# A two-layer decoder step: cache pages loaded one by one from SyncE, and half of the key products in three fp32r passes

## The chip, the core and the metric

The kernel runs on one core of a Trainium2 chip. The core has TensorE (matmuls into PSUM), VectorE, ScalarE and GpSimd, SyncE as a queue that issues transfers, and 16 DMA engines between DRAM and SBUF. The metric is the device time in microseconds of one execution. In the profile TensorE is PE (PEld its weight loads), VectorE DVE, ScalarE ACT, GpSimd POOL and SyncE SP.

## What is computed

One inference step of a decoder with two layers, for a prompt of 1024 tokens and a sample group of 8 sequences with 4 new tokens each. Every layer norms and projects its input, runs three branches (a pooling mixer, a short convolution and latent attention), gates them and projects back. The change touches the sample group's attention over its cache, 64 pages of 128 tokens for each sequence, found through a page table:

```
def step(carry, pt):
    m, lsum, acc = carry
    lat = cache_latent[layer, pt]            # (8, 128 tokens, 128 channels)
    krp = cache_krope[layer, pt]             # (8, 128 tokens, 32)
    kn = key_nope(lat, w_uk, kn_g)           # rmsnorm of (lat @ w_uk), 4 heads x 64
    s = attn_scores(qn, qr, kn, krp)
    m_new = jnp.maximum(m, jnp.max(s, axis=-1))
    corr = jnp.exp(m - m_new)
    p = jnp.exp(s - m_new[..., None])
    lsum = lsum * corr + jnp.sum(p, axis=-1)
    acc = acc * corr[..., None] + jnp.einsum('bhqk,bkc->bhqc', p, lat.astype(jnp.float32))
    return (m_new, lsum, acc), None
```

## The kernel before

Each layer has three stages. The projections with the preparation of queries and keys come first, then the cache stage, then the prompt's attention, whose first tiles overlap the end of the cache stage; the output projection follows. The first is ordered by a scheduler, the cache stage and the prompt's attention in the order in which the code writes them.

The cache stage (`sample_attn`, L481) goes over 16 units, each half of one sequence's pages: 32 pages, 4096 tokens. A unit has 8 steps of 512 tokens (`tau` counts all 128 steps). Both layouts of a unit's pages come by indirect gathers from GpSimd (`rows`, L490): `latc` for the keys, two units ahead, `lat` for the values, and the rotary keys `kr`. VectorE turns 512 columns of `latc` a step, in blocks of 32, three steps ahead (`T`, L519). `K` (L529) is the key product: for each of four groups of 128 tokens one fp32 matmul of the turned block with `WK`, 272 columns wide: 256 key channels for the norms and 16 score columns, into which the queries are folded. In the program an fp32 matmul is one row; on the chip it is two instructions. ScalarE squares the 256 columns and copies the 16 (`nope`, L545); each `kproj` buffer in PSUM (there are three, of two groups each) is free when both have read it. GpSimd adds the halves of the squares (`tree`), VectorE sums them (`red`), and per unit the inverse root (`lnexp`, `newton`), the scaling, the rotary part, the maximum, the exponential and the value product `pv` (L614) follow, one and two units behind.

Of the 8 buffers of the pool `big` (`slot`, L58) the stage uses those that the gate rows `mixM` and `mixA` of the prompt and the prompt's first head leave. In layer 0, seven blocks of `w_ada` for later modulation are loaded whole beside the units (`ada_step`, L630). In the prompt's attention, `load_qk` and `load_v` (L816, L822) fetch one head from DRAM, and `qk_part` and `v_part` split it into two fp32r parts on ScalarE and GpSimd; `warm` (L846) does that for head 0 in the last units. A product in three passes is `mm3` (L213): high by high, high by low, low by high, each an fp32r matmul with its own weights.

## Time and profile before

| | us |
|---|---|
| three runs, median | 1607.45 |
| lowest and highest | 1606.56, 1608.36 |
| the profiled execution's own time | 1606.35 |
| its span, first to last instruction | 1604.6 |
| TensorE busy | 1547.2 (96%) |
| VectorE busy | 1122.6 (70%) |
| ScalarE busy | 790.4 (49%) |
| GpSimd busy | 743.8 (46%) |

The busy times are sums over the whole span; a stretch is read from its own rows. A matmul's recorded duration holds its way through the array, and neighbours overlap, so the distance of two starts is what a matmul takes in a row of them. SyncE's transfers are not counted as busy; their rows in order of time show the issue alone, and the data land later.

### The profile page before, as it was taken

To read this page: it belongs to the slowest core of one execution; us is meant where nothing else is said; L and a number is where in the kernel's file an instruction comes from. 1 tells how busy PE (TensorE), PEld (TensorE's weight loads), DVE (VectorE), ACT (ScalarE), POOL (GpSimd) and SP (SyncE) were. 2 spreads that over 40 slices of the span, in tenths; PEclk is the share of its full clock that TensorE was granted. 3 is DMA by queue.
4 is the path that set the end of the run, shared out by engine and by line. 5 is a ranking of instruction groups with operands and counts; after the bars stand their busy time and mean duration, and the time that the engine had idled before them with its cause. 6 is when DMAs were issued, how large, how long until landed. Compare 5 with 4: busy or idle time off the path is not lost.

```text
span 1604.6 us, 28029 instructions
## 1 busy us (share of the span) xinstructions
PE 1547.2 (96%) x10576; PEld 1386.7 (86%) x10576; DVE 1122.6 (70%) x2131; ACT 790.4 (49%) x1935; POOL 743.8 (46%) x594
## 2 busy tenths in 40 slices
PE   4899999999999999999998999999999999989999
PEld 2799999977777888889987999998888888878999
DVE  7746755578888888684268477546899999967522
ACT  4444444365555556583145344334666665657500
POOL 3311211276666667364444021223777777746520
PEclk8999999999999999999999999999999999999999
DMA  9202223567777775213522112314666666541242
GB/s 385 56 20 70 64 77 73 171 273 281 297 285 281 287 272 192 59 47 121 202 90 70 41 40 73 78 60 153 243 260 260 261 261 251 206 125 48 68 160 82
DMA packets 79557, 254.48 MB, mean 159 GB/s; under 512 B 25472, under 2 KB 49088, under 8 KB 69184
## 3 DMA queue, kind: packets, MB, share of 16 engines
q0 software_dynamic: 13824, 151.00, 23.7%
q1 hardware_dynamic: 65600, 101.69, 20.0%
q8 instruction: 85, 1.39, 0.3%
q14 instruction: 48, 0.39, 0.1%
HBM read 231.87 MB, written 20.80 MB: 157 GB/s over the span
## 4 chain that ended last, share of the span: by engine, by line
PE 87%; DVE 6%; DMA 2%; issue 2%; ACT 1%; POOL 1%; SPq 0%; DVEq 0%; POOLq 0%; ACTq 0%
PE kproj L541 29%; PE po L620 4%; PE ropesc L569 3%; PE outa L198 2%; PE outa L200 2%; PE outa L196 2%; PE PTp L166 2%; PE rawps L216 2%; PE rawps L214 2%; PE rawps L215 2%; PE pvo L214 1%; DMA src<-qscr 1%; PE outb L200 1%; PE outb L196 1%; PE outb L198 1%
## 5 line engine op out<-in xcount | busy, mean ns | idle before, releaser
L541 PE MATMUL kproj<-WK,lT 128*128 128x272 f32 x2048 | 497.5, 397 | 3.9 <-DVE lT L525 3.9
L541 PEld LDWEIGHTS kproj<-WK,lT 128*128 128x128 f32 x2048 | 378.9, 190 | 90.0 <-issue 15.9
L101 ACT ACTIVATE sq<-kproj 128x512 f32<-128x512 f32 x512 | 305.3, 597 | 252.0 <-PE kproj L541 248.9
L104 POOL TENSOR_TENSOR t<-sq 128x512 f32<-128x512 f32 x256 | 322.3, 1274 | 138.3 <-ACT nope L547 108.3
L104 POOL TENSOR_TENSOR wt<-wraw,wt 128x1024 fp32r<-128x1024 f32 x44 | 106.9, 2431 | 312.4 <-ACT wt L116 308.3
L525 DVE STREAM_TRANSPOSE lT<-latc 128x512 f32<-128x512 f32 x256 | 177.4, 694 | 35.7 <-PE kproj L541 31.9
L557 DVE TENSOR_REDUCE ms<-t 128x16 f32<-128x512 f32 x256 | 167.0, 652 | 10.8 <-POOL t L104 10.5
L116 ACT CAST wt<-wraw 128x1024 fp32r<-128x1024 f32 x44 | 46.7, 1064 | 125.1 <-PE outb L200 81.2
L547 ACT COPY nope<-kproj 128x32 f32<-128x32 f32 x512 | 93.0, 182 | 0.6 <-DMA qscr<-qkm 0.6
L104 POOL TENSOR_TENSOR kn<-raw,ones 128x128 f32<-128x128 f32 x18 | 13.0, 723 | 163.6 <-DVE raw L104 88.2
L1365 PE MATMUL zma<-hT,wt 128*128 128x352 f32 x192 | 49.9, 366 | 26.8 <-ACT hT L1145 18.9
L569 PEld LDWEIGHTS ropesc<-BD,krT 128*128 128x128 f32 x512 | 66.8, 192 | 4.7
L886 DVE TENSOR_REDUCE pmx<-sc 128x1 f32<-128x128 f32 (+3 forms) x64 | 48.1, 751 | 26.7 <-PE pvo L166 23.5
L1365 PEld LDWEIGHTS zma<-hT,wt 128*128 128x128 f32 x192 | 36.9, 214 | 33.6 <-ACT hT L1145 21.6
L104 DVE TENSOR_TENSOR PT<-PTp,PT 128x512 fp32r<-128x512 f32 (+2 forms) x96 | 50.2, 551 | 21.8 <-ACT PT L929 20.8
L929 ACT CAST PT<-PTp 128x512 fp32r<-128x512 f32 (+2 forms) x96 | 42.8, 481 | 45.9 <-PE PTp L166 45.4
L569 PE MATMUL ropesc<-BD,krT 128*128 128x64 f32 x512 | 64.0, 268 | 0.0
L620 PE MATMUL po<-lat,p 128*32 128x128 f32 x2048 | 62.5, 274 | 0.0
L104 POOL TENSOR_TENSOR qkT<-src,qkT 96x512 fp32r<-96x512 f32 x32 | 40.9, 1279 | 33.6 <-ACT qkT L832 33.3
L620 PEld LDWEIGHTS po<-lat,p 128*32 128x32 f32 x2048 | 53.9, 110 | 2.1
L104 POOL TENSOR_TENSOR nope<-nope,rs 128x512 f32<-128x512 f32 x32 | 35.2, 1100 | 35.2 <-DVE rs L581 35.2
L101 ACT ACTIVATE P<-sc,pmx 128x128 f32<-128x128 f32 (+3 forms) x64 | 47.9, 749 | 6.9 <-DVE pmx L886 6.3
(452 smaller groups left out, 3906.2 us busy)
## 6 DMA issues: line engine op xcount, KB each, us to landing
wada<-in_w_ada SPq DMA_DIRECT2D x11, 2048.0 KB, 8.0
wraw<-in_w_in SPq DMA_DIRECT2D x32, 512.0 KB, 3.8
wraw<-in_w_out SPq DMA_DIRECT2D x14, 512.0 KB, 5.1
qscr<-qkm SPq DMA_DIRECT2D x32, 192.0 KB, 2.1
xo<-in_xT SPq DMA_DIRECT2D x8, 528.0 KB, 5.3
xscr<-xn SPq DMA_DIRECT2D x8, 528.0 KB, 3.0
xo<-xscr SPq DMA_DIRECT2D x8, 528.0 KB, 5.6
vscr<-Vm SPq DMA_DIRECT2D x16, 256.0 KB, 2.0
```

The costliest lines, as they stand in the source:

```text
L101: s.activation(out, in_, func, **k)
L104: (e or v).tensor_tensor(out, x, y, op)
L196: te.matmul(outs[n], wt[:, 0, k, :], hi[:, n * CH:(n + 1) * CH], start=(k == 0), stop=False)
L198: te.matmul(outs[n], wt[:, 0, k, :], lo[:, n * CH:(n + 1) * CH], start=False, stop=False)
L200: te.matmul(outs[n], wt[:, 1, k, :], hi[:, n * CH:(n + 1) * CH], start=False, stop=(k == 7))
L525: v.transpose(h.lT[q], h.latc[:, 512 * q:512 * q + 512])
L541: te.matmul(kp[:, i, 0:KPC], lT[:, sl], wk, start=True, stop=True)
L547: s.copy(h.nope[:, t0:t0 + 2].rearrange("p n h t -> p n (h t)"), kp[:, :, 256:KPC])
L557: v.tensor_reduce(h.ms[:, 4 * q:4 * q + 4, :].rearrange("p n (h o) -> p (n h) o", o=1), t32, AX.X, ALU.add)
L569: te.matmul(h.pr[:, o:o + 64], h.krT[c][:, 128 * k:128 * k + 128], BD[:, h.b, :], start=True, stop=True)
L620: te.matmul(h.po[32 * j:32 * j + 32, 0:128], p[:, 16 * t:16 * t + 32], h.lat[:, t * 128:(t + 1) * 128], start=(q == 0), stop=(q == 7))
L1365: te.matmul(o, zmw[j][:, i // 2, k, :], (lo if i == 1 else hi)[:, c], start=(k == 0 and i == 0), stop=(k == 7 and i == 1))
```

## The change

Pages no longer come by gathers of a whole unit. `pages(tau)` issues four transfers on SyncE, each one page of 128 rows of 1 KB: 128 numbers of the page by channels (the layout that the key product wants as weights) and 128 by tokens (the layout for the values), which the host has laid side by side in DRAM. The page's number comes from the table `pgt` in SBUF into a register of SyncE, eight numbers in one instruction every second step, and a further instruction multiplies it to an address. The transposes `T` and the gathers of `latc` and `lat` are gone; the gather of `kr` stays, in another order of rows. In steps 1, 3, 5 and 7 of a unit ScalarE and GpSimd split the block into two fp32r parts (`cast`, three steps ahead) and the key product runs as `mm3`. In these steps the squares are summed by VectorE alone, from the full width; in the others VectorE copies the 16 score columns instead of ScalarE. `newton` runs on GpSimd, with one square on ScalarE. Pages are issued five steps ahead, in buffers of 16 pages. To free buffers, the gate rows `mixM` and `mixA` go to DRAM (`mscr`) after the projections and come back during the prompt's attention. `w_ada` comes in eight pieces, one a step. Head 0's value split moves behind the stage, and the splits of head 1 come one tile later.

```
-    WKR = cp.tile([128, 2, 256], F32R, name="WKR")
-    WK = [cp.tile([128, KPC], F32, name=f"WK{i}") for i in range(2)]
+    pgt = cp.tile([1, 2 * NB * 32], I32, name="pgt")
+    WUK = cp.tile([128, 2, KPC], F32R, name="WUK")
...
+    NTAU = NU * NSTEP
+    THREE = (1, 3, 5, 7)
+    AHEAD, CAST = 5, 3
...
+        krs, sums = [], []
+        numbers = []
+
+        def pages(tau):
+
+            if tau >= NTAU:
+                return
+            u, q = divmod(tau, NSTEP)
+            if q == 0:
+                H[u] = P()
+                H[u].b, H[u].pg = u // 2, []
             h = H[u]
-            h.lat = flat(slot(f"lat{l}_{u}"), 4096)
-            rows(u, h.lat, "lat")
+            if q % 4 == 0:
+                h.pg.append(flat(slot(f"pg{l}_{u}_{q}"), 4096).rearrange("p (n x) -> p n x", n=16))
+            if q % 2 == 0:
+                _, values = nc.values_load_multi_w_load_instructions(
+                    pgt[0:1, 4 * tau:4 * tau + 8], engines=[mybir.EngineType.SP], min_val=0, max_val=NPOOL - 1,
+                    skip_runtime_bounds_check_because="entries of the page table are numbers of pages of the pool")
+                numbers[:] = values
+            for i in range(4):
+                nc.sync.dma_start(h.pg[q // 4][:, 4 * (q % 4) + i, :],
+                                  a["pages"][l][bass.ds(numbers.pop(0), 1)].rearrange("o p x -> p (o x)"))
...
+        def turned(h, q):
+            return h.pg[q // 4][:, 4 * (q % 4):4 * (q % 4) + 4, 0:128]
+
+        def cast(tau):
+            u, q = divmod(tau, NSTEP)
+            if tau < NTAU and q in THREE:
+                h = H[u]
+                h.hl = getattr(h, "hl", {})
+                hi = pool.tile([128, 4, 128], F32R, tag="hi", name="hi", bufs=3)
+                lo = pool.tile([128, 4, 128], F32R, tag="lo", name="lo", bufs=3)
+                s.copy(hi, turned(h, q))
+                sub(lo, turned(h, q), f(hi), g)
+                h.hl[q] = hi, lo
...
             for i in range(2):
                 t = 2 * j + i
-                sl = slice(t * 128, (t + 1) * 128)
-                te.matmul(kp[:, i, 0:KPC], lT[:, sl], wk, start=True, stop=True)
+                if q in THREE:
+                    hi, lo = h.hl[q]
+                    mm3(kp[:, i, 0:KPC], hi[:, t], lo[:, t], wr[:, 0], wr[:, 1])
+                else:
+                    te.matmul(kp[:, i, 0:KPC], turned(h, q)[:, t], wk, start=True, stop=True)
+            if q in THREE and j:
+                h.hl.pop(q)
             act(h.sq[:, 2 * j:2 * j + 2, :], kp[:, :, 0:256], AF.Square)
             return kp
...
         def nope(h, q, j, kp):
             t0 = 4 * q + 2 * j
-            s.copy(h.nope[:, t0:t0 + 2].rearrange("p n h t -> p n (h t)"), kp[:, :, 256:KPC])
-
-        def tree(h, q):
-            sv = h.sq.rearrange("p n (h x d) -> p (n h) x d", h=NH, x=2)
-            t32 = pool.tile([128, 16, 32], F32, tag="t32", name="t32", bufs=3)
-            add(t32, sv[:, :, 0, :], sv[:, :, 1, :], g)
-            halves.append((h, q, t32))
+            dst = h.nope[:, t0:t0 + 2].rearrange("p n h t -> p n (h t)")
+            if q in THREE:
+                s.copy(dst, kp[:, :, 256:KPC])
+            else:
+                v.tensor_copy(dst, kp[:, :, 256:KPC])
+
+        def add_up(h, q):
+
+            x = h.sq.rearrange("p n (h d) -> p (n h) d", h=NH)
+            if q not in THREE:
+                t32 = pool.tile([128, 16, 32], F32, tag="t32", name="t32", bufs=2)
+                add(t32, x[:, :, 0:32], x[:, :, 32:64], g)
+                x = t32
+            sums.append((h, q, x))
 
         def red():
-            h, q, t32 = halves.pop(0)
-            v.tensor_reduce(h.ms[:, 4 * q:4 * q + 4, :].rearrange("p n (h o) -> p (n h) o", o=1), t32, AX.X, ALU.add)
+            h, q, x = sums.pop(0)
+            v.tensor_reduce(h.ms[:, 4 * q:4 * q + 4, :].rearrange("p n (h o) -> p (n h) o", o=1), x, AX.X, ALU.add)
 
...
         def lnexp(h):
             h.t0 = keep.tile([128, 32, NH], F32, tag="ta", name="ta", bufs=2)
+            h.rs = keep.tile([128, 32, NH], F32, tag="rs", name="rs", bufs=2)
             act(h.t0, h.ms, AF.Ln, scale=1.0 / NOPE, bias=epsT)
             act(h.t0, h.t0, AF.Exp, scale=-0.5)
-
-        def newton(h):
-            h.rs = keep.tile([128, 32, NH], F32, tag="rs", name="rs", bufs=2)
-            mul(h.rs, h.t0, h.t0)
-            v.tensor_scalar(h.ms, h.ms, -0.5 / NOPE, -0.5 * EPS, ALU.mult, ALU.add)
-            mul(h.rs, h.rs, h.ms)
-            v.scalar_tensor_tensor(h.rs, h.rs, 1.5, h.t0, ALU.add, ALU.mult)
+            act(h.rs, h.t0, AF.Square)
+
+        def newton(h, e=g):
+            e.tensor_scalar(h.ms, h.ms, -0.5 / NOPE, -0.5 * EPS, ALU.mult, ALU.add)
+            mul(h.rs, h.rs, h.ms, e)
+            if e is v:
+                v.scalar_tensor_tensor(h.rs, h.rs, 1.5, h.t0, ALU.add, ALU.mult)
+            else:
+                e.tensor_scalar_add(h.rs, h.rs, 1.5)
+                mul(h.rs, h.rs, h.t0, e)
...
             if not odd:
-                if q == 3:
-                    A.w = ada_load(*ada[c])
+                if q == 0:
+                    A.w = flat(slot(f"wada{c}"), 4096).rearrange("p (k n) -> p k n", k=8)
+                nc.sync.dma_start(A.w[:, q], a["w_ada"][ada[c]][:, q])
...
+        for tau in range(AHEAD):
+            pages(tau)
         gather_kr(0)
-        gather_kr(1)
+        add(WK[0][:, 0:256], f(WUK[:, 0, 0:256]), f(WUK[:, 1, 0:256]))
+        v.tensor_copy(WK[1][:, 0:256], WK[0][:, 0:256])
+        v.tensor_copy(WKR[1][:, :, 0:256], f(WUK[:, :, 0:256]))
         new_wk(0)
-        T(0)
-        T(1)
-        T(2)
+        for tau in range(CAST):
+            cast(tau)
...
-            T(tau + 3)
+            pages(tau + AHEAD)
             kp = K(h, q, 0)
+            cast(tau + CAST)
             nope(h, q, 0, kp)
-            if tau > 1:
+            if q % 2 == 0 and sums:
                 red()
...
             kp = K(h, q, 1)
-            tree(h, q)
+            add_up(h, q)
             nope(h, q, 1, kp)
+            if q % 2:
+                red()
             if hp is not None:
                 if q == 1:
-                    lnexp(hp)
+                    newton(hp)
...
-                elif q == 3:
+                elif q == 1:
                     rowsum(hpp, u - 2)
+                elif q == 2:
                     for i in range(8):
                         pv(hpp, u - 2, i)
-                elif q == 4:
+                elif q == 3:
                     pvend(hpp, u - 2)
                     hpp = None
-            if q == 5:
-                gather_n(u)
-                gather_c(u + 2)
-            elif q == 7:
-                gather_kr(u + 2)
+            if q == 3:
+                gather_kr(u + 1)
...
         def warm(u, q):
-            if (u, q) == (13, 6):
+            if (u, q) == (14, 7):
                 first.append(slot("src0"))
                 load_qk(0, flat(first[0], 3 * SEQ))
                 load_v(0, flat(first[0], 3 * SEQ))
-            elif (u, q) in QKQ:
-                qk_part(0, QKQ.index((u, q)), s)
-            elif (u, q) in VQ:
-                v_part(0, VQ.index((u, q)))
-                if (u, q) == VQ[1]:
-                    first.clear()
-                    SRC.clear()
+            elif u == 15 and q in (3, 5, 6, 7):
+                qk_part(0, (3, 5, 6, 7).index(q), s)
+
+        def warm_v():
+            for i in range(2):
+                v_part(0, i)
+            first.clear()
+            SRC.clear()
...
+            warm_v()
             load_qk(1, src)
             load_v(1, src)
+            mixM = slot("mixM")
+            for h in range(NH):
+                nc.sync.dma_start(mixM[:, h, :], mscr[l][:, 4 + h, :])
...
+                if x == 8:
+                    mixA = slot("mixA")
+                    for i in range(4):
+                        nc.sync.dma_start(mixA[:, i, :], mscr[l][:, i, :])
...
+                    z = y if hh else y - 1
+                    if 0 <= z < 4:
+                        qk_part(hh + 1, z, s)
+                    elif 4 <= z < 6:
+                        v_part(hh + 1, z - 4)
+                    if z == 3 and hh + 2 < NH:
                         load_qk(hh + 2, src)
-                    if y == 5 and hh + 2 < NH:
+                    if z == 5 and hh + 2 < NH:
                         load_v(hh + 2, src)
...
+        for h in range(NH):
+            nc.sync.dma_start(mscr[l][:, 4 + h, :], mixM[:, h, :])
+        mixM = None
         for i in range(2):
             branch_a(l, i, hc, wts, mixA, up)
+            nc.sync.dma_start(mscr[l][:, i, :], mixA[:, i, :])
         for i in range(2):
             branch_b(l, i, hc, wts, mixA, up)
+            nc.sync.dma_start(mscr[l][:, 2 + i, :], mixA[:, 2 + i, :])
...
-    d["ptr"] = np.tile(i["page_table"].reshape(2 * NB, NPAGES // 2).T, (4, 1))
-    lat = i["cache_latent"].reshape(DEPTH, NPOOL, 32, 4, 128)
-    d["lat"] = lat.transpose(0, 1, 3, 2, 4).reshape(DEPTH * NPOOL * 4, 4096)
-    d["latc"] = lat.reshape(DEPTH, NPOOL, PAGE, 4, 32).transpose(0, 1, 3, 2, 4).reshape(DEPTH * NPOOL * 4, 4096)
-    kr = i["cache_krope"].reshape(DEPTH, NPOOL, 8, 4, 4, ROPE)
-    d["kr"] = kr.transpose(0, 1, 3, 2, 4, 5).reshape(DEPTH * NPOOL * 4, 1024)
+    table = i["page_table"].reshape(2 * NB, NPAGES // 2)
+    d["pgt"] = table.reshape(1, -1)
+    d["ptr"] = np.repeat(table.reshape(2 * NB, 8, 4).transpose(2, 1, 0).reshape(32, 2 * NB), 4, axis=0)
+    lat = i["cache_latent"]
+    d["pages"] = np.concatenate([lat.transpose(0, 1, 3, 2), lat], axis=3)
+    d["kr"] = i["cache_krope"].reshape(DEPTH * NPOOL * 4, 1024)
```

On SyncE, in layer 0, before: three of the seven loads of `w_ada` that stand in the cache stage (`wada`), then those for the prompt's attention (`src`, `wuvs`), with nothing between them.

```order
L229 DMA wada_2_4605<-in_w_ada 128x4096
L229 DMA wada_3_5029<-in_w_ada 128x4096
L229 DMA wada_4_5453<-in_w_ada 128x4096
L820 DMA src_5734<-qscr_111 96x2x1024
L824 DMA src_5734<-vscr_113 128x8x128
L757 DMA wuvs<-in_w_uv 128x512
L820 DMA src<-qscr_111 32x2x1024
```

After, in the same stage, around the change from step 3 to step 4 of a unit's pages (`pg_7` is unit 7; ISA is the multiplication, TENSOR_LOAD the load of eight registers; `wada` is a piece of `w_ada`):

```order
L511 ISA
L511 DMA pg_7_0_5035<-in_pages 128x256
L666 DMA wada_4918<-in_w_ada 128x512
L506 TENSOR_LOAD pgt
L511 ISA
L511 DMA pg_7_4_5178<-in_pages 128x256
L511 ISA
L511 DMA pg_7_4_5178<-in_pages 128x256
```

Between two pieces of `w_ada` there are now four page transfers, each with an instruction ahead of it, and a register load every second time.

On TensorE, before, units 1 to 2 of layer 0, a step being four rows of `kproj`:

```order
L541 MATMUL kproj<-WK_90,lT 128x272 x12
L166 MATMUL pm<-ident,mx 16x128
L541 MATMUL kproj<-WK_90,lT 128x272 x4
L601 MATMUL pm<-ident,M 128x16
L541 MATMUL kproj<-WK_90,lT 128x272 x12
L569 MATMUL ropesc<-BD,krT 128x64 x4
L541 MATMUL kproj<-WK_90,lT 128x272 x4
```

After, steps 2 and 3 of unit 9 (`hi` and `lo` are the parts of the block, WUK and WK its weights; the last three rows come four times):

```order
L556 MATMUL kproj<-WK_2884,pg_9_0_5709 128x272 x4
L592 MATMUL ropesc<-BD,krs 128x64 x4
L647 MATMUL po<-pg_7_0_5035,p_2883 32x128 x16
L647 MATMUL po<-pg_7_4_5178,p_2883 32x128 x16
L214 MATMUL kproj<-WUK,hi 128x272
L215 MATMUL kproj<-WUK,hi 128x272
L216 MATMUL kproj<-WUK,lo 128x272
```

The value products of an older unit stand one step earlier, directly behind step 2's products, and the products of step 3 are three rows each.

On GpSimd, before, the end of unit 9 in layer 0 (`t` is the addition of halves, and the three gathers stand between):

```order
L104 TENSOR_TENSOR t_4822<-sq 128x512
L104 TENSOR_TENSOR t_4851<-sq 128x512
L492 DMA lat_9_4854<-in_lat,idx_86 128x4096
L492 DMA latc_11_4856<-in_latc,idx_86 128x4096
L104 TENSOR_TENSOR t_4873<-sq 128x512
L104 TENSOR_TENSOR t_4900<-sq 128x512
L492 DMA krs<-in_kr,idx_86 128x1024
```

After, unit 9 with the small operations of `newton` (`ms`, `rs`) and the subtraction of `cast` (`lo`):

```order
L104 TENSOR_TENSOR t_5919<-sq 128x512
L602 TENSOR_SCALAR ms<-ms 128x128
L104 TENSOR_TENSOR rs<-rs,ms 128x128
L607 TENSOR_SCALAR rs<-rs 128x128
L104 TENSOR_TENSOR rs<-rs,ta 128x128
L104 TENSOR_TENSOR lo<-pg_9_4_5852,hi 128x512
L104 TENSOR_TENSOR t_5994<-sq 128x512
L104 TENSOR_TENSOR nope<-nope,rs 128x512
L520 DMA krs<-in_kr,idx_86 128x1024
```

Two gathers are gone; subtractions and the four small operations have come between the additions.

## Rows read from the trace of the kernel before

**Rows 1.** The page: engines' busy time (share, instructions); DMA queue's packets, MB, share.
```profile
PE 1547.2 (96%) x10576; PEld 1386.7 (86%) x10576; DVE 1122.6 (70%) x2131; ACT 790.4 (49%) x1935; POOL 743.8 (46%) x594
...
q1 hardware_dynamic: 65600, 101.69, 20.0%
```

**Rows 2.** The two cache stages: busy us (instructions) by engine, clock, DMA share, GB/s.
```profile
320.80:635.10 314.30, 314.24 (x2330) 252.19 (x2330) 270.94 (x460) 189.63 (x567) 222.32 (x190) 1.00 0.69 270
1111.00:1408.50 297.50, 296.92 (x2190) 246.77 (x2190) 266.55 (x441) 186.76 (x559) 221.84 (x190) 1.00 0.60 236
```

**Rows 3.** Who waited for whom, TensorE: us in total, times, longest us.
```profile
PE kproj L541 <- DVE lT L525: 3.9, 2, 2.0
```

**Rows 4.** In order of time, TensorE, one unit of layer 1: start us, us, what.
```profile
1168.74 2.05 PE L541 MATMUL kproj<-WK,lT 128*128 128x272 f32 x8
1170.63 1.00 PE L569 MATMUL ropesc<-BD,krT 128*128 128x64 f32 x8
...
1187.68 2.05 PE L541 MATMUL kproj<-WK,lT 128*128 128x272 f32 x8
```

**Rows 5.** In order of time, TensorE: the prompt's value products, 256 columns.
```profile
704.24 0.28 PE L214 MATMUL pvo<-PT,VR 128*128 128x256 f32 x1
...
704.60 0.28 PE L214 MATMUL pvo<-PT,VR 128*128 128x256 f32 x1
```

**Rows 6.** In order of time, TensorE: the projection at 416 columns.
```profile
99.95 0.35 PE L214 MATMUL rawps<-wqh,hT 128*128 128x416 f32 x1
...
100.53 0.35 PE L214 MATMUL rawps<-wqh,hT 128*128 128x416 f32 x1
```

**Rows 7.** Groups by line and form, layer 1's cache stage: busy us, mean ns | idle.
```profile
L104 POOL TENSOR_TENSOR t<-sq 128x512 f32<-128x512 f32 x127 | 159.7, 1274 | 59.9 <-ACT nope L547 48.7 <-DVE lT L525 10.3 <-DVE nope L104 0.3
L101 ACT ACTIVATE sq<-kproj 128x512 f32<-128x512 f32 x255 | 151.9, 596 | 119.2 <-PE kproj L541 117.8 <-issue 0.2
L525 DVE STREAM_TRANSPOSE lT<-latc 128x512 f32<-128x512 f32 x127 | 88.0, 694 | 11.3 <-PE kproj L541 10.3 <-DMA latc<-in_latc,idx 1.0
L557 DVE TENSOR_REDUCE ms<-t 128x16 f32<-128x512 f32 x126 | 82.0, 651 | 6.5 <-POOL t L104 6.5
L547 ACT COPY nope<-kproj 128x32 f32<-128x32 f32 x255 | 46.2, 181 | 0.0
...
L104 DVE TENSOR_TENSOR rs<-ta 128x128 f32<-128x128 f32 x15 | 28.0, 1864 | 0.0
...
L104 POOL TENSOR_TENSOR nope<-nope,rs 128x512 f32<-128x512 f32 x15 | 16.5, 1100 | 14.4 <-DVE rs L581 14.4
...
L492 POOL DMA_INDIRECT krs<-in_kr,idx x14 | 13.3, 951 | 2.2 <-DVE krT L561 2.1 <-issue 0.2
...
L104 POOL TENSOR_TENSOR qkT<-src,qkT 96x512 fp32r<-96x512 f32 x4 | 5.1, 1272 | 0.0
...
L832 ACT CAST qkT<-src 96x512 fp32r<-96x512 f32 x4 | 2.5, 618 | 0.0
```

**Rows 8.** In order of time, SyncE's queue: start us, us, what.
```profile
28.82 0.33 SPq L1158 DMA_DIRECT2D wqraw<-in_w_q  x1
29.20 0.42 SPq L229 DMA_DIRECT2D wada<-in_w_ada  x1
29.67 0.42 SPq L1355 DMA_DIRECT2D cpk<-in_cpk  x1
30.14 0.43 SPq L1356 DMA_DIRECT2D ptr<-in_ptr  x1
```

**Rows 9.** One line's instructions: ns min/median/max; here TensorE's sequencer.
```profile
L541 PEldq EVENT_SEMAPHORE  x495: 51/51/197, 320.7 to 1406.1; - x165
```

**Rows 10.** DMA issues: count, KB each, median us from issue to landing.
```profile
out_newconv<-vB SPq DMA_DIRECT2D x4, 1.0 KB, 1.4
```

**Rows 11.** Two stretches at the start of the prompt's attention, columns as in Rows 2.
```profile
644.00:656.00 12.00, 9.28 (x44) 7.67 (x44) 7.37 (x14) 6.97 (x15) 6.65 (x7) 0.72 0.12 31
1417.00:1429.00 12.00, 8.38 (x36) 6.56 (x34) 6.30 (x14) 6.23 (x13) 5.22 (x6) 0.72 0.18 52
```

More of the change, by code (lines that the diff above doesn't have):

```diff
@@ L287, in load_small_w @@
         split(r.wuq[:, 0], r.wuq[:, 1], wq)
-        split(WKR[:, 0], WKR[:, 1], w[:, 768:1024])
-        for i in range(2):
-            v.tensor_copy(WK[i][:, 0:256], w[:, 768:1024])
+        split(WUK[:, 0, 0:256], WUK[:, 1, 0:256], w[:, 768:1024])
         w = pool.tile([128, 8, 128], F32, tag="wraw", name="wuvraw", bufs=2).rearrange("p a b -> p (a b)")[:, 0:512]
@@ L486, in sample_attn @@
         pbuf = [keep.tile([128, 528], F32, tag=f"p{i}", name=f"p{i}") for i in range(2)]
+        WK = [pool.tile([128, KPC], F32, tag=f"WK{i}", name=f"WK{i}") for i in range(2)]
+        WKR = [WUK, pool.tile([128, 2, KPC], F32R, tag="WKR", name="WKR")]
         H = {}
-        krs, halves = [], []
-        def rows(u, dst, src):
-            off = bass.IndirectOffsetOnAxis(ap=idx[l][:, u:u + 1], axis=0)
-            g.indirect_dma_start(out=dst, out_offset=None, in_=a[src], in_offset=off)
-        def gather_c(u):
-            if u < NU:
-                h = H[u] = P()
-                h.b = u // 2
-                h.latc = flat(slot(f"latc{l}_{u}"), 4096)
-                rows(u, h.latc, "latc")
-        def gather_n(u):
-            h = H[u]
-            h.lat = flat(slot(f"lat{l}_{u}"), 4096)
-            rows(u, h.lat, "lat")
+        krs, sums = [], []
[7 more added lines that the diff above has]
+                H[u].b, H[u].pg = u // 2, []
+            h = H[u]
+            if q % 4 == 0:
[8 more added lines that the diff above has]
+                                  a["pages"][l][bass.ds(numbers.pop(0), 1)].rearrange("o p x -> p (o x)"))
         def gather_kr(u):
@@ L511, in gather_kr @@
                     krs.append(slot("krs"))
-                H[u].kr = krs[0][:, u % 4, 0:1024]
-                rows(u, H[u].kr, "kr")
+                H[u].kr = krs[0][:, u % 2, 0:1024]
+                off = bass.IndirectOffsetOnAxis(ap=idx[l][:, u:u + 1], axis=0)
+                g.indirect_dma_start(out=H[u].kr, out_offset=None, in_=a["kr"], in_offset=off)
         def new_wk(b):
             if b < NB:
-                v.tensor_copy(WK[b % 2][:, 256:KPC], S.qa[:, b].rearrange("p h t -> p (h t)"))
-        def T(tau):
-            if tau >= NU * NSTEP:
-                return
-            h, q = H[tau // NSTEP], tau % NSTEP
-            h.lT = getattr(h, "lT", {})
-            h.lT[q] = pool.tile([128, 512], F32, tag="lT", name="lT", bufs=4)
-            v.transpose(h.lT[q], h.latc[:, 512 * q:512 * q + 512])
-            if q == NSTEP - 1:
-                h.latc = None
+                qa, w = S.qa[:, b].rearrange("p h t -> p (h t)"), WKR[b % 2]
+                v.tensor_copy(WK[b % 2][:, 256:KPC], qa)
+                split(w[:, 0, 256:KPC], w[:, 1, 256:KPC], qa)
+        def turned(h, q):
[10 more added lines that the diff above has]
+                h.hl[q] = hi, lo
         def K(h, q, j):
@@ L566, in rope @@
                 h.pr = (psr if h is H.get(NU - 1) else psm)("ropesc")
[L567 to L569 removed]
+            for k in range(4 * c, 4 * c + 4):
+                te.matmul(h.pr[:, 64 * k:64 * k + 64], h.krT[:, 128 * k:128 * k + 128], BD[:, h.b, :], start=True, stop=True)
         def lnexp(h):
             h.t0 = keep.tile([128, 32, NH], F32, tag="ta", name="ta", bufs=2)
+            h.rs = keep.tile([128, 32, NH], F32, tag="rs", name="rs", bufs=2)
             act(h.t0, h.ms, AF.Ln, scale=1.0 / NOPE, bias=epsT)
             act(h.t0, h.t0, AF.Exp, scale=-0.5)
[L576 to L581 removed]
+            act(h.rs, h.t0, AF.Square)
[7 more added lines that the diff above has]
+                mul(h.rs, h.rs, h.t0, e)
         def scale(h):
@@ L641, in ada_step @@
             elif q == 5:
-                A.mg = pool.tile([128, 512], F32, tag="adamg", name="adamg")
+                A.mg = krs[0][:, 3, 0:512]
                 s.copy(A.mg, A.ps)
@@ L657, in sample_attn @@
             v.memset(pbuf[i][:, 512:528], 0.0)
-        for tau in range(NSTEP * NU):
+        for tau in range(NTAU):
             u, q = divmod(tau, NSTEP)
@@ L708, in sample_attn @@
             ada_step(u, q)
-            if q == 4 and u % 2 == 1 and u // 2 + 2 < NB + 1 and u > 1:
+            if q == 4 and u % 2 == 1 and 1 < u < NU - 1:
                 new_wk(u // 2 + 1)
@@ L722, in tail @@
             rope(h, 1)
+            h.kr = h.krT = A.mg = None
+            krs.clear()
             rowsum(hp, u - 1)
@@ L1045, in _build @@
     xscr = dp.tile([128, 8, TOK], F32, name="xscr")
+    mscr = [dp.tile([128, 8, TOK], F32, name=f"mscr{l}") for l in range(DEPTH)]
     qscr = [dp.tile([128, 2, 3, SEQ], F32, name=f"qscr{l}") for l in range(DEPTH)]
```

59 lines of the change are left out of this document (26 added, 33 removed).

## The prediction, made before the changed kernel ran

> **What bounds the kernel now.** I read the page first, then the stretches of the two cache stages, then who waited for whom, then one unit in order of time. A unit is half of one sequence's pages (32 pages, 4096 keys); a step is four pages, so a unit has 8 steps and a layer 16 units. The page shows TensorE busy for 96% of the span [rows 1]. The two stretches are the cache stages: 314.3 us in layer 0 and 297.5 us in layer 1, 611.8 us together, and TensorE is busy for 611.2 us of that, at a granted clock of 1.00, its 2.4 GHz level; VectorE, the next, is busy for 537.5 [rows 2]. The key products wait 3.9 us in the whole run, at the stages' starts [rows 3]. So inside the stage nothing but TensorE's own queue sets the time. In order of time, a unit of layer 1 takes 18.94 us (1168.74 to 1187.68); eight key matmuls take 1.89 us, 0.236 each [rows 4]. The program's fp32 product is two such instructions, so 0.472 us; a step has four products.
>
> **TensorE: what the three passes give.** In steps 1, 3, 5 and 7 a product becomes three fp32r matmuls of 272 columns, each with its own weights. The nearest rows are the prompt's value products, the same three lines at 256 columns, where three take 0.36 us (704.24 to 704.60) [rows 5], and the projection at 416 columns, where three take 0.58 us (99.95 to 100.53) [rows 6]. Between them, 272 columns lie at 0.127 each, 0.381 for three. A product saves 0.091 us; 16 products a unit and 32 units make 512, **46.6 us**, and a unit of layer 1 would take 18.94 - 1.46 = 17.48 us.
>
> **Does another compute engine take over?** Each unit gains 4 casts on ScalarE and 4 subtractions on GpSimd; it loses 8 transposes on VectorE, 4 of the 8 halving additions and two of its three gathers; the small square-root step goes from VectorE to GpSimd, half the score copies from ScalarE to VectorE. From [rows 7]: ScalarE 16 squares at 0.596, 8 copies at 0.181, 4 casts at 0.618 and some 1.7 of small work, 15.1 us. GpSimd 4 additions at 1.274, 4 subtractions at 1.272 (the row of qkT, the same operation), one scaling at 1.1, one gather near 0.95 and four operations of 128 elements, each between 0.32 (a quarter of 1.274) and 1.27: 13.5 to 17.3 us. VectorE was at 266.6 / 15.7 units = 17.0 [rows 2]; less 8 transposes at 0.694 and about 2.8 of the square-root step (its first product alone was 1.864), plus 8 copies of at most 0.28 and four reductions of twice the size (4 x 0.65): 13 to 14 us. All stay below 17.48, and casts run three steps ahead, so I cost them at nothing; without that cover GpSimd would be first, at its upper bound, 0.2 us a unit short of TensorE.
>
> **SyncE: what the pages cost.** Before, SyncE issues hardly anything in the stage: seven loads of w_ada in layer 0 and the first loads for the prompt. After, each unit has 32 page transfers, each behind a register instruction, and 4 loads of 8 registers from the table, all in one queue; the w_ada pieces of layer 0 (8 in each of 7 units) stand in the same queue. Whatever a register load takes, all page transfers behind it wait, and TensorE waits for those. The terms:
> - A transfer of 128 rows issued behind another one: starts at 29.20, 29.67 and 30.14, so 0.47 us [rows 8]. The kind with an address from a register is not in the trace.
> - The register instruction: the nearest row is an instruction that a sequencer handles alone, 0.051 us [rows 9]. Together 0.52 us a page.
> - A load of 8 registers: no row. Below, it costs what any sequencer instruction costs, 0.05; above, it is a round trip to memory that cannot be dearer than the smallest transfer's whole way, 1.4 us from issue to landing [rows 10]. I take the middle, 0.73, since it is neither of the two: 0.091 a page.
> So a page costs 0.611 us of SyncE. The 16 engines that move the bytes are no bound: the hardware queue moved 101.69 MB in 20.0% of 16 engines' span [rows 1], 317 GB/s while busy, so 128 KB take 0.41 us.
>
> The first 16 pages of a layer go into a buffer that is free before the stage. The other 496 in each layer make 992 x 0.611 = 606.1 us, plus 56 pieces of w_ada x 0.47 = 26.3: **632.4 us of SyncE against 611.8 us of stage** before, and against 611.8 - 46.6 = 565.2 us that TensorE would need. By this SyncE is the bound and the stages get 20.6 us longer; the gain of the three passes turns into TensorE's waiting. The buffers do not add to it: a page buffer is released by the value products of an older unit, 6 to 10 steps before its new pages are needed.
>
> The Trainium skill (DMA: Bandwidth & Descriptors, section Latency and other measured facts) gives a floor of about 600 ns for a tensor_load; with it the sum would be 992 x 0.595 + 26.3 = 616.5 us, an estimate, and no change within the measurement. No run here shows a register load yet.
>
> **The rest.** At the start of the prompt's attention, behind the transfer of head 1, TensorE is busy for only 17.7 of the 24 us of two stretches, and at 0.72 of the clock (part of the time at its 1.2 GHz level) [rows 11]: 6.3 us idle and, at 0.28 of 17.7, 4.9 us lost to the clock. The first use of head 1 is now one tile later, and no gather of 2 MB is in flight beside its load. Bounds: nothing, or all of the 11 us; against it stands that head 0's value split moves here from the cache stage. I take 6 us of gain. Writing the gate rows to DRAM and reading them back (4 MB each way and layer) lies beside projections and prompt tiles; I cost it at nothing, and if the reload came late at head 0's first gate, at 2 to 4 us a layer.
>
> **Sum.** The profiled execution took 1606.35 us; the median of the runs is 1.1 above. 1606.35 + 20.6 - 6 = 1621.0, on the median **1622 us**.
>
> **Rivals.** (1) TensorE stays the bound. That holds if a page costs at most about 0.546 us (the 565.2 us, less 26.3, over 992; in layer 0, with the w_ada pieces, a little less): a register load under 0.21. For it: the lower bounds, and the transfer at 28.82, which had waited and takes 0.38 to the next start [rows 8]. Against: 0.47 is already 86% of that. It gives 1606.35 - 46.6 - 6 + 1.1 = 1555 us, and up to 16 more if VectorE, which now frees half the product buffers, is late by 0.5 us a unit. (2) The register load costs its upper bound, 1.4: a page 0.695, SyncE 992 x 0.695 + 26.3 = 715.7 us, the stages +103.9: 1705 us, slower by far more than the forecast. It decides from a load of 0.61 us on: there 992 x 0.597 + 26.3 equals the old stages plus the 6 us. A page's rule points further this way: the Trainium skill (Runtime: NRT & Kernel Launch, section Instruction fetch mechanics) puts a register load at about 200 ns for each register, by which 8 would be 1.6 us and the total some 1729, an estimate that no run here shows. (3) GpSimd takes over, its four small operations at 1.27 and its gather late: 18.1 us a unit, 32 x 0.84 = 27 us gained, 1575 us.
>
> **How the numbers follow.** SyncE as the bound with a load between about 0.2 and 1.1 us: 0.55, of which 0.15 end faster than before, 0.06 the same and 0.34 slower, its own range 1571 to 1668. TensorE still the bound 0.25; the dear register load 0.15; GpSimd 0.05. Faster by over 0.2% (what a measurement of this kernel can tell from no change): 0.15 + 0.25 + 0.05 = 0.45; same 0.06; slower 0.34 + 0.15 = 0.49. The range leaves out half of the dear case and the last bit of the cheap one: 1553 to 1690.
>
> **What would show it.** In the changed profile: the register load's duration on SyncE and the distance of two page transfers (0.52 without it); key products that wait for a page's transfer while GpSimd, ScalarE and VectorE have slack; a unit of 19.6 us in layer 1 and up to 2 us more in layer 0's units with w_ada. If instead units take 17.5 us and the key products wait for nothing, the SyncE step is wrong. If three passes are further apart than 0.381 us with no wait, the TensorE step is. If the key products wait for casts or for a free product buffer, the step that costs the other engines at nothing is.

## The result, and the profile after the change

The changed kernel takes 1661.31 us (median of four runs, 1656.27 to 1673.89), the one before in the same comparison 1607.20: 1.0348 times as long, interval 1.0289 to 1.0406. The forecast was 1622, the range 1553 to 1690, its likeliest case SyncE as the bound: 15 us of loss, where 54 were measured. The profiled execution is the longest of the four (1673.89 us, a span of 1672.1); the same kernel profiled again, as one of the runs below, took 1663.65. I measure a stage from the start of its first key product to the start of its last, and count units from 0:

| us | layer 0 | layer 1 | all the rest | sum |
|---|---|---|---|---|
| before | 313.7 | 297.1 | 995.5 | 1606.35 |
| after | 356.8 | 320.6 | 996.5 | 1673.89 |
| after, again | 356.3 | 318.1 | 989.3 | 1663.65 |

All of the loss lies in the two cache stages: 43 and 21 to 24 us. The two stretches after, as [rows 2] shows them before (length, then busy us of PE, PEld, DVE, ACT, POOL, then clock, DMA share, GB/s):

```profile
319.50:676.60 357.10, 314.34 (x2586) 260.77 (x2586) 223.38 (x408) 211.14 (x520) 220.13 (x220) 0.98 0.80 244
1157.70:1478.50 320.80, 290.64 (x2447) 252.09 (x2447) 209.94 (x390) 208.80 (x513) 220.19 (x220) 0.99 0.75 225
```

TensorE, busy all the time before, now stands idle for 43 and 30 us, and no other compute engine is busy for more than 69% of either stretch. So something that this view doesn't count, or an order, holds TensorE. First SyncE: the register load and the page transfer (ns shortest, median, longest):

```profile
L506 SPq TENSOR_LOAD <-pgt x128: 520/528/902, 183.8 to 1460.3; - x128
...
L511 SPq DMA_DIRECT2D pg<-in_pages x1024: 332/333/2847, 184.8 to 1467.8; - x171
```

Then its queue in order of time (start, length, pages), 8 pages between two loads and 16 in a row, and below it 10 pages of the first experiment's kernel, which needs no number:

```profile
1234.67 4.01 SPq L511 DMA_DIRECT2D pg<-in_pages  x8
...
1229.81 8.87 SPq L511 DMA_DIRECT2D pg<-in_pages  x16
```
```profile
1190.36 4.72 SPq L506 DMA_DIRECT2D pg<-in_pages  x10
```

Eight pages between two loads: (4.01 - 0.333) / 7 = 0.525 us a page. The row of 16 holds one load more, so from the last page ahead of a load to the first behind it it takes 8.87 - 0.333 - 14 x 0.525 = 1.19 us; with that a page costs 0.608 us, a unit 19.5. By a sum over SyncE's records, issues that take over 0.5 us instead of 0.333 (up to 2.85) add 1.1 to 1.3 us a unit, pauses of 0.34 us another 0.3: SyncE needs 20.8 to 21.1 us a unit in layer 1 and 22.9 in layer 0, where the pieces of w_ada come in. It paces layer 0 from unit 2 on. In layer 1 it starts ahead and loses its lead; by counting the pages, these are the first issues for units 4 and 14 and the products that use them:

```profile
1212.72 1.07 SPq L511 DMA_DIRECT2D pg<-in_pages  x1
...
1230.30 0.62 PE L556 MATMUL kproj<-WK,pg 128*128 128x272 f32 x2
...
1423.30 0.98 SPq L511 DMA_DIRECT2D pg<-in_pages  x1
...
1432.44 0.62 PE L556 MATMUL kproj<-WK,pg 128*128 128x272 f32 x2
```

17.6 us ahead, then 9.1; from unit 9 on the lead stays between 8.6 and 10.5 us, as the pages take 2.9 us to land and are cast three steps ahead. (Both of these issues are long ones.) Units 3 to 8 take 19.77 us each, units 9 to 14 20.7. The waits say the same, in layer 0 (410 to 660 us), then in layer 1 at 1340 to 1453; the last two rows are of 1221 to 1319.9, five units in which no row of this kind stands (total, times, longest):

```profile
ACT hi L538 <- DMA pg<-in_pages: 46.5, 27, 4.5
...
ACT hi L538 <- DMA pg<-in_pages: 9.1, 14, 1.0
...
PE kproj L556 <- DVE nope L568: 5.3, 10, 0.7
...
PE pm L628 <- DVE M L625: 2.4, 5, 0.5
```

In these five units no page is late, and yet each takes 19.77 us, more than the 18.94 of before. What TensorE waits for there is VectorE, (5.3 + 2.4) / 5 = 1.5 us a unit; in order of time around one such wait:

```profile
1263.30 0.19 DVE L568 COPY nope<-kproj 128x32 f32<-128x32 f32 x1 [2.90 <-ACT sq L101]
1263.41 1.21 DVE L581 TENSOR_REDUCE ms<-sq 128x16 f32<-128x1024 f32 x1
1264.54 0.68 DVE L104 TENSOR_TENSOR nope<-nope,ropesc 128x512 f32<-128x512 f32 x1
1265.13 0.18 DVE L568 COPY nope<-kproj 128x32 f32<-128x32 f32 x1
...
1265.37 0.96 PE L556 MATMUL kproj<-WK,pg 128*128 128x272 f32 x3 [0.37 <-DVE nope L568]
```

VectorE had been idle for 2.90 us. But its two copies, each of which frees a product buffer, stand 1.83 us apart, with a reduction of double size and an addition between them in its queue, and the next product waits for the second.

The last unit of layer 1 takes 25.0 us (23.7 in the second profile). There the first loads for the prompt's attention, head 0's, stand between the pages in SyncE's queue, and one cast waits 7.0 us for a page (1453 to 1478.3):

```profile
ACT hi L538 <- DMA pg<-in_pages: 8.0, 2, 7.0
```

### The profile page after: what moved, and what is told of

Its sections match the earlier page's. It is cut to its first block, busy times and chain, and to the rows that moved or that the text cites. A ratio compares the mean times of both kernels' runs of the same rounds, so it can differ in the third digit from the quotient of the medians.

```text
span 1672.1 us, 32516 instructions
## 1 busy us (share of the span) xinstructions
PE 1545.7 (92%) x11088; PEld 1405.3 (84%) x11088; DVE 1020.2 (61%) x2027; ACT 838.9 (50%) x1855; POOL 733.8 (44%) x650
## 5 line engine op out<-in xcount | busy, mean ns | idle before, releaser
L556 PE MATMUL kproj<-WK,pg 128*128 128x272 f32 x1024 | 276.1, 411 | 57.6 <-DVE nope L568 52.4
L556 PEld LDWEIGHTS kproj<-WK,pg 128*128 128x128 f32 x1024 | 186.6, 194 | 103.2 <-DVE nope L568 66.4
L104 POOL TENSOR_TENSOR lo<-pg,hi 128x512 fp32r<-128x512 f32 x128 | 164.8, 1287 | 241.6 <-ACT hi L538 174.7
L104 POOL TENSOR_TENSOR t<-sq 128x512 f32<-128x512 f32 x128 | 163.0, 1273 | 0.2
L581 DVE TENSOR_REDUCE ms<-t 128x16 f32<-128x512 f32 x128 | 86.8, 678 | 114.6 <-POOL t L104 113.0
L581 DVE TENSOR_REDUCE ms<-sq 128x16 f32<-128x1024 f32 x128 | 154.8, 1209 | 0.0
L538 ACT CAST hi<-pg 128x512 fp32r<-128x512 f32 x128 | 78.8, 616 | 83.3 <-DMA pg<-in_pages 82.9
L214 PE MATMUL kproj<-WKR,hi 128*128 128x272 f32 x256 | 88.6, 346 | 2.5 <-DVE nope L568 2.5
L214 PE MATMUL kproj<-WUK,hi 128*128 128x272 f32 x256 | 87.4, 341 | 2.5 <-DVE nope L568 2.5
L215 PE MATMUL kproj<-WKR,hi 128*128 128x272 f32 x256 | 74.4, 290 | 0.0
L216 PE MATMUL kproj<-WKR,lo 128*128 128x272 f32 x256 | 74.2, 290 | 0.0
L215 PE MATMUL kproj<-WUK,hi 128*128 128x272 f32 x256 | 74.1, 290 | 0.0
## 6 DMA issues: line engine op xcount, KB each, us to landing
wada<-in_w_ada SPq DMA_DIRECT2D x4, 2048.0 KB, 14.8
```

The costliest lines, as they stand in the source:

```text
L104: (e or v).tensor_tensor(out, x, y, op)
L214: te.matmul(out, lh, rh, start=start, stop=False)
L215: te.matmul(out, lh, rl, start=False, stop=False)
L216: te.matmul(out, ll, rh, start=False, stop=stop)
L538: s.copy(hi, turned(h, q))
L556: te.matmul(kp[:, i, 0:KPC], turned(h, q)[:, t], wk, start=True, stop=True)
```

## The experiments

Theories: S, SyncE's issue paces layer 0 and the end of layer 1; V, where it does not, the order of TensorE, ScalarE and VectorE does; D, the bytes in flight do. Medians, ratios to the kernel before in the same comparison, and stages of the profiled execution:

| run | us | ratio (95%) | layer 0 | layer 1 | units 3 to 8, layer 1 |
|---|---|---|---|---|---|
| e1_fixed | 1621.61 | 1.0086 (1.0069 to 1.0103) | 330.0 | 302.9 | 19.22 |
| e2_two | 1650.81 | 1.0268 (1.0250 to 1.0285) | 347.6 | 311.5 | 19.09 |
| e3_wada | 1659.42 | 1.0307 (1.0282 to 1.0331) | 348.5 | 316.5 | 19.77 |
| e4_nope | 1662.40 | 1.0327 (1.0301 to 1.0353) | 358.2 | 318.8 | 19.40 |
| e5_load32 | 1643.68 | 1.0237 (1.0199 to 1.0275) | 346.6 | 312.6 | 19.72 |
| e6_fixed_nope | 1602.00 | 0.9964 (0.9952 to 0.9976) | 327.2 | 291.2 | 18.50 |
| e7_fixed_two | 1611.39 | 1.0029 (1.0005 to 1.0053) | 318.3 | 301.4 | 19.09 |
| e8_best | 1642.50 | 1.0234 (1.0211 to 1.0256) | 334.1 | 309.2 | 19.40 |
| e9_best2 | 1654.33 | 1.0290 (1.0273 to 1.0307) | 359.0 | 304.9 | 19.15 |
| e10_pairs | 1613.00 | 1.0034 (1.0018 to 1.0050) | 327.9 | 294.3 | 18.68 |
| e11_again | 1663.65 | one run | 356.3 | 318.1 | 19.77 |
| e12_passes | 1602.74 | 0.9968 (0.9959 to 0.9978) | 311.2 | 298.1 | 18.84 |

**e1: pages from fixed addresses.**

```diff
-            if q % 2 == 0:
-                _, values = nc.values_load_multi_w_load_instructions(
...
-                                  a["pages"][l][bass.ds(numbers.pop(0), 1)]...
+                                  a["pages"][l][4 * tau + i:4 * tau + i + 1]...
```

> Pages come from fixed addresses: no table, no register load, no multiplication (this leaves out the look-up of the page numbers). Theory S (SyncE's issue sets the pace of layer 0 and of the second half of layer 1; where it does not, TensorE's waits for VectorE hold a unit at 19.8 us): a page costs SyncE about 0.47 us, a unit 15.0 and some 1.5 of long issues, so pages are ahead everywhere but the 19.8 us stay: stages 2 x 317 instead of 357 and 321, total about 1617 us. Theory P (SyncE sets everything, the 19.8 us too): units near 17.5, total about 1560 us. Theory D (the bytes in flight on the DMA engines, not the issue, delay the pages): the bytes are the same, so about 1661 us.

1621.61 us: leaving the look-up out saves 40 us. S's total of 1617 is near that partly by luck: it had 317 us for either stage, and they took 330.0 and 302.9. A page is now (4.72 - 0.43) / 9 = 0.477 us of SyncE (row above; an issue here lasts 0.43). A unit of layer 1 takes 19.22 us, not the 19.77 that S kept. The product that waited for VectorE's copy in the changed kernel waits for ScalarE's here, although the edit touches neither (1160 to 1400 us):

```profile
PE kproj L551 <- ACT nope L561: 4.9, 12, 0.4
```

Why that is so is not shown. At 0.55 us a unit it can make 8 of the 18 us that layer 1 gains, so the 40 us need not be SyncE's alone. The bytes are the same, so D falls as the cause of the 40 us. Fixed pages lie one behind another in DRAM, but they don't land sooner for that: in e6, with the same addresses, a page takes 3.8 us to land in layer 0 and 3.0 in layer 1 (median), in the changed kernel 3.2 and 2.5 (345 to 650 and 1180 to 1440 us). P falls, since without the look-up the kernel is still slower than before.

**e2: the pages without the three passes.**

```diff
-    THREE = (1, 3, 5, 7)
+    THREE = ()
...
-            if q in THREE:
-                s.copy(dst, kp[:, :, 256:KPC])
-            else:
-                v.tensor_copy(dst, kp[:, :, 256:KPC])
+            s.copy(dst, kp[:, :, 256:KPC])
```

> Every key product as one fp32 product, no casts, all score copies on ScalarE; the pages as in the changed kernel. Theory S: layer 0 stays at SyncE's pace (units of 23 us); in layer 1 TensorE starts at 18.9 us a unit, uses up the lead sooner and then goes at SyncE's 21.0: total 1655 to 1668 us, as with the three passes. Theory V (the loop of TensorE, ScalarE and VectorE sets the pace everywhere): back to units of 18.9 us, about 1607 us.

1650.81: 4 us below S's lower end, far from V's 1607. Everything but the passes costs 43 us, and the passes with their copies on VectorE come to another 10 instead of a gain. Layer 1 goes at 19.09 to unit 12, where the lead has shrunk to 6.0 us: the products no longer need their pages three steps ahead.

**e3: w_ada in whole blocks.**

```diff
-                nc.sync.dma_start(A.w[:, q], a["w_ada"][ada[c]][:, q])
+                    nc.sync.dma_start(A.w, a["w_ada"][ada[c]])
```

> Each block of w_ada in one transfer instead of eight, the rest as changed. Theory S: SyncE loses 49 issues of about 0.47 us and the waits around them, layer 0 goes from 23.0 to 21.0 us a unit: about 1633 us. Theories V and D: same bytes and same loop, 1661 us.

1659.42, a miss. Layer 0 gains 8 us in the profile and the median next to nothing. The queue says why: a transfer waits for the one eight places ahead of it (they share a semaphore), and a block takes long to land. SyncE's waits at 340 to 640 us:

```profile
SPq L511 <- DMA wada<-in_w_ada: 14.8, 4, 4.1
```

That row names four of the waits; of the seven blocks, six are followed by a pause of 3.1 to 4.2 us eight issues later. What the pieces had cost in issues comes back as a wait: SyncE's queue still takes 22.5 us a unit and sets the pace, though S had only counted its issues.

**e4: all score copies on ScalarE.** The second half of e2's diff.

> All score copies back on ScalarE, the rest as changed. Theory S: layer 0 unchanged; units 3 to 8 of layer 1 go from 19.8 to about 18.3 us because no product buffer waits for VectorE, and SyncE's 21.0 us take over sooner: total within 1655 to 1663 us. Theory V: every unit loses 1.5 us, about 1613 us.

1662.40, within S's range. Units 2 to 4 of layer 1 take 18.4 us instead of 19.8, so VectorE's copies are what held TensorE there; the lead is used up at unit 5, and SyncE's pace follows. One cause hides the other.

**e5: one register load of 32 numbers.**

```diff
-            if q % 2 == 0:
+            if tau % 8 == 0:
...
-                    pgt[0:1, 4 * tau:4 * tau + 8], ...
+                    pgt[0:1, 4 * tau:4 * tau + 32], ...
```

> One register load of 32 page numbers a unit instead of four of 8. Theory F (a load has a fixed price, about 0.65 us from page to page beside the page's own 0.526): SyncE needs 1.95 us a unit less, 19.0 in layer 1, so units stay at TensorE's 19.8 through the whole layer; layer 0 goes from 23.0 to 21 to 21.5: about 1630 us. Theory R (the price goes by the register): a load of 32 takes some 2.1 us or more, nothing is saved, about 1661 us.

1643.68, between the two. The load decides for R:

```profile
L506 SPq TENSOR_LOAD <-pgt x32: 1860/1867/2774, 184.9 to 1418.1; - x32
```

32 registers take 1.867 us, 8 took 0.528: (1.867 - 0.528) / 24 = 0.056 a register and 0.08 for the load. What is saved are the fixed part and the pauses of three loads, 0.5 to 0.65 us a unit. In layer 0 that makes 8 to 10 us, and the stage gained 10.2. In layer 1 SyncE sets only the later units, and of the 8.0 us gained there some 4 are of this kind; others come from units 3 to 7, which take 19.5 us instead of 19.77, and from the last unit, 22.5 instead of 25.0. F was wrong.

**e6 and e7: fixed addresses, copies on ScalarE, with three passes and without.** e1's diff with the second half of e2's; e6 has the cast behind the copy, e7 has `THREE = ()`.

```diff
-            cast(tau + CAST)
             nope(h, q, 0, kp)
+            cast(tau + CAST)
```

> Fixed page addresses as in the first run (the look-up is left out), all score copies on ScalarE and the cast behind the copy. Theory S with V (SyncE first, and behind it the product buffers that VectorE frees late): a unit of layer 1 takes 18.4 us instead of 19.2, layer 0's likewise: about 1597 us. If VectorE's copies have nothing to do with it, 1621 us as in the first run.

> Fixed page addresses (the look-up is left out), every key product as one fp32 product, all score copies on ScalarE: what is left when SyncE no longer bounds and no pass is split. TensorE's 19.0 us a unit in layer 1 as before the change: about 1610 us. Against the run with three passes and ScalarE's copies this gives the worth of the passes: 23 us if each change from fp32 to fp32r costs the 0.2 us that the rows show (four a unit), 47 us if the forecast's price holds.

e6 takes 1602.00 us (expected 1597), so 20 of the us that e1 had left are VectorE's copies and the place of the cast. e7 takes 1611.39 (1610), 9 more than e6 and not the 23 or 47 that were expected. In layer 1 the passes give 19.09 - 18.50 = 0.59 us a unit, and e6 still waits 0.8 us a unit there for the maximum (first row, 1160 to 1410 us). In layer 0 they lose 9 us. There casts need their pages earlier, and SyncE, with w_ada, has nothing to spare: the cast waits 22 times for a page, and SyncE itself 30.4 us for earlier transfers to land (the other rows, 360 to 640 us):

```profile
PE pm L620 <- DVE M L617: 10.5, 13, 0.8
...
ACT hi L533 <- DMA pg<-in_pages: 38.5, 22, 3.3
...
SPq L506 <- DMA pg<-in_pages: 14.5, 18, 1.8
SPq L506 <- DMA wada<-in_w_ada: 9.5, 19, 2.0
SPq L658 <- DMA pg<-in_pages: 6.4, 5, 1.8
```

So once the look-up is gone, the time to land, D's concern, comes back in layer 0. In the changed kernel such waits make 10.5 us there (330 to 670 us).

**e8: a version with the look-up that should win.** e5's load, e4's copies, e6's place of the cast, and

```diff
+                    g.dma_start(A.w, a["w_ada"][ada[c]])
...
-                elif q == 7:
-                    bcast(hp, pu)
             kp = K(h, q, 1)
...
                 elif q == 7:
+                    bcast(hp, pu)
                     expo(hp, pu)
```

> The look-up is kept; one load of 32 numbers a unit, the blocks of w_ada whole and from GpSimd's queue, all score copies on ScalarE with the cast behind them, and the broadcast of the maximum behind the second half of the step's products. By theories F, S and V a unit takes SyncE 18.8 us and TensorE 17.7 to 18.4, in layer 0 another 2.5 in every second unit for w_ada: about 1585 to 1600 us, faster than before the change. If the long issues of SyncE grow with the pace, or GpSimd's transfer delays the pages, 1610 to 1640.

1642.50, a miss, for the reason that e5 gave: the sum used F. SyncE needs 20.1 to 20.3 us a unit. But while the lead lasts, TensorE runs as fast as the passes allow; the first row is layer 1's unit 2, the second its unit 10:

```profile
1161.10:1178.80 17.70, 17.68 (x163) 15.81 (x162) 12.85 (x16) 13.01 (x40) 13.28 (x15) 1.00 0.78 234
1315.30:1336.00 20.70, 18.52 (x163) 15.76 (x163) 12.63 (x16) 13.66 (x41) 13.85 (x15) 1.00 0.75 230
```

**e9: four of 32 pages from ScalarE's queue.** On top of e8; `last_pages` loads four numbers and issues four transfers on ScalarE.

```diff
+            if q == 2:
+                last_pages(u)
```

> As the run before it (e8), but four of a unit's 32 pages are issued from ScalarE's queue, behind its copies of step 2, where TensorE has the value products; SyncE loads 28 numbers and ScalarE 4. Theory S: SyncE's unit falls by 4 x (0.526 + 0.056) = 2.3 us to 17.9, about what TensorE needs (17.7 with no wait), ScalarE's rises by 2.4 to some 17: about 1642 - 2 x 15 x 1.9 = 1590, within 1585 to 1605 us, faster than before the change. If ScalarE's issues wait for earlier transfers and hold the squares, or the bytes bound, 1625 us or more.

1654.33, a miss: 12 us slower than e8. Layer 1 gains 4 us, layer 0 loses 25. The transfers of the two queues share the eight semaphores in the order of the program, so SyncE waits for ScalarE's four as well, by a sum over its records for 32 of 60 us; SyncE's waits at 340 to 640 us:

```profile
SPq L513 <- DMA pg<-in_pages: 56.4, 37, 5.5
SPq L513 <- PE po L655: 16.2, 10, 2.9
```

**e10: three passes in pairs of steps.**

```diff
-    THREE = (1, 3, 5, 7)
+    THREE = (2, 3, 6, 7)
```

> As the run with fixed addresses and ScalarE's copies (e6; the look-up is left out), but the three passes run in steps 2, 3, 6 and 7, so TensorE goes from fp32 to fp32r products twice a unit instead of four times. If each such change costs the 0.2 us of the rows, a unit of layer 1 goes from 18.50 to 18.1 us and the total from 1602 to about 1590 us. If the 0.2 us belongs to something else (the first weights of a step, a buffer), it stands four times a unit as before: 1602 us. ScalarE, with two dense steps in a row, could add a wait of up to 0.4 us a unit.

1613.00, above either forecast. A unit takes 18.68 instead of 18.50, so fewer changes gain nothing. The 0.2 us was my misreading of the rows; in the changed kernel a change looks so (the first row holds three instructions, the last of which starts at 1263.11):

```profile
1262.65 0.85 PE L556 MATMUL kproj<-WK,pg 128*128 128x272 f32 x3
1263.14 0.49 PE L214 MATMUL kproj<-WUK,hi 128*128 128x272 f32 x1
1263.47 0.29 PE L215 MATMUL kproj<-WUK,hi 128*128 128x272 f32 x1
```

The first fp32r row starts 0.03 us behind the last fp32 row and the next one 0.33 later; together 0.36, which is 0.23 for the fp32 instruction and 0.125 for an fp32r one. A change is free. That the run is 11 us slower than e6 is not settled. TensorE waits up to 2.0 us for the column maximum (14.8 us, 14 times, in layer 1; 10.5 in e6), which now stands among dense steps; in the profiles 4 us of the difference lie in the stages and 5 outside them.

**e11: the changed kernel again.** No edit.

> The changed kernel unaltered, for the spread between executions, which was 1656 to 1674 us with the profile in the slowest. Theory S: the pages' own distance (0.526 us) and the load (0.53 us) repeat to the ns; what differs is the number and length of SyncE's long issues (1.2 to 1.5 us a unit) and where layer 1's lead runs out: 1655 to 1670 us.

1663.65, with page distance and load as before. The 10 us to the other profile are 3 in the stages and 7 in the rest. The lead runs out at unit 10 instead of 9.

**e12: the passes on the kernel before.** Gathers and transposes stay; `cast` takes the turned block, `new_wk`, `K`, `newton` and the sums are as in the changed kernel, all copies on ScalarE.

```diff
+                t = h.lT.pop(q).rearrange("p (n x) -> p n x", n=4)
+                s.copy(hi, t)
+                sub(lo, t, f(hi), g)
...
-            T(tau + 3)
             kp = K(h, q, 0)
             nope(h, q, 0, kp)
+            cast(tau + 2)
...
             nope(h, q, 1, kp)
+            T(tau + 3)
```

> The other half of the change alone, on the kernel before: gathers and transposes stay, no page goes through SyncE, and the three passes come in (steps 1, 3, 5 and 7, cast two steps ahead from the turned block), with the squares of these steps summed by VectorE alone and the small square-root step on GpSimd; ScalarE keeps all score copies; the rotary keys are gathered one unit ahead instead of two. Theory S with V: SyncE has nothing to do, no product buffer waits for VectorE, so a unit is TensorE's 17.7 us (the 17.48 of the forecast and some 0.2 at each change from fp32 to fp32r, less the 0.3 by which the products are quicker), at most 18.5 where GpSimd (16.3 us by its rows) or VectorE (16.7) is late: 1575 to 1600 us, faster than both. If the passes themselves are worth nothing, 1607 us; if GpSimd, with three gathers and the casts, sets the pace, 1610 us or more.

1602.74, 0.3% faster than before (0.9968) and less than expected. Units of layer 1 alternate between 17.65 us, what TensorE needs, and 20.0, where the low part comes late from GpSimd, or VectorE's maximum does. Layer 1, 1120 to 1410 us:

```profile
PE kproj L216 <- POOL lo L104: 9.5, 11, 1.3
PE pm L166 <- DVE mx L621: 5.0, 7, 0.8
```

So this kernel beats both kernels of the case, the one before by little; most of what the passes give is still lost in queues.

## Why the prediction was right, and where it was wrong

- **SyncE as the bound: right.** A page takes 0.525 us (forecast 0.52), with its share of a load 0.608 (0.611). The load's middle value, 0.73, was near the 0.66 that it adds, which is luck: no row bore on it, and it lay between 0.05 and 1.4. e1 shows that without the look-up 40 us are gone, e2 that the passes gain nothing behind SyncE. The sign of 19.6 us a unit in layer 1 came out in its first half, 19.77, by luck too: there VectorE's queue was the cause.
- **The size was short by 39 us.** The stages took 674 to 677 us, not 632.4. The term mis-sized is the page's: to the 19.5 us of pages and loads in a unit, as forecast, long issues and pauses add 1.4 to 1.6. In layer 0 (356.8 us, where the sum has 496 x 0.611 + 26.3 = 329.4) they make about 25 of the 27 us that are missing. In layer 1 (320.6, where the sum has 303.1) they act from unit 9 on, 7 of 17.5 us; 5 more are the last unit's, with head 0's loads among the pages, and 5 those of the units that TensorE paces. The trace of before has long issues as well, in a row 10 us behind those of [rows 8]: four issues of 64 rows each take 0.93 us apiece, not 0.47. Whether their cause is the same is not shown.

```profile
39.91 3.71 SPq L1467 DMA_DIRECT2D poolw<-in_pool_w  x4
```

  The pieces of w_ada were sized right (0.46 each).
- **Other engines at nothing: wrong.** Their busy times came out as forecast or below (ScalarE 13.1, GpSimd 13.9, VectorE 13.6 us in a unit of layer 1), and still VectorE's queue delays TensorE by 1.5 us a unit where SyncE doesn't: the price that I had only put into rival 1, and three times as high. I compared busy times with the unit, and a buffer is freed not by an idle engine but by one instruction's place in its queue. e4 shows it: 19.8 to 18.4. The rest is the wait for the maximum: with its broadcast moved as well, e8 has units of 17.7.
- **The passes' own gain: right.** 18.94 - 1.46 = 17.48 was the forecast for a unit; e12 shows 17.65 and e8 17.7 where nothing waits. An fp32 product takes 0.459 us (its instructions start 0.2295 apart; I had divided a stretch that held the step to the next product), three passes 0.37 to 0.38, so a product saves 0.08 to 0.09 where 0.091 was forecast. No run got this gain for a whole stage.
- **The rest of the program, -6 us:** +1.0 in the first profile, -6.2 in the second, so between the bounds.
- **The rivals.** Rival 1 fell by its own point: it needed a load under 0.21 us. Rival 2, 1705 us, came nearest of them, but its cause, a load of 1.4 us, isn't there. Rival 3 fell too: GpSimd is busy for 13.9 us of a unit. The Trainium skill (DMA: Bandwidth & Descriptors, section Latency and other measured facts) has a floor of about 600 ns for a tensor_load; a load of 8 took 528. The Trainium skill (Runtime: NRT & Kernel Launch, section Instruction fetch mechanics) has some 200 ns a register; the slope here is 56. By neither would the time have come out.
- **Slips in the sums.** By its own terms SyncE as the bound with a load of 0.2 us gives 1557 us, not 1571, and rival 1's limit is (565.2 - 26.3) / 992 = 0.543 us a page, not 0.546. Neither bears on the outcome.

## What to carry to other kernels

Where many small transfers replace a few gathers, the queue that issues them is an engine: count its instructions per unit, allow for issues longer than the shortest that the trace shows, and compare with the time of the loop before asking about bytes. When a copy that frees a buffer goes to an engine with time to spare, look at what stands ahead of it in that engine's queue, not at its busy share. And a lead that shrinks steadily, while the loop's time doesn't change yet, is a bound that has not arrived: read a long stage at its start and at its end.

## What the runs showed of the hardware beyond that

- A load of numbers from SBUF into SyncE's registers takes 0.08 us and 0.056 for each register (8: 0.528, 32: 1.867, and 28 in e9: 1.643), so larger loads save little. On ScalarE a load of 4 takes 0.308 (e9).
- About one page issue in 20 takes 0.5 to 2.7 us instead of 0.333 (20 to 22 of 416, units 2 to 14 of a layer, in both profiles of the changed kernel); at fixed addresses one in 11 is over 0.5 us, where 0.43 is usual. What causes it stayed open.
- In these compiled programs the transfers of SyncE and ScalarE take turns on eight semaphores, so one waits for the one eight places ahead of it in the program (e3: 3.1 to 4.2 us behind a block of w_ada; e9: about half of the 56.4 us in layer 0, behind ScalarE's). A large transfer or a second queue in a dense stream of small ones cost waits by that.
